# A smaller descriptor scratch for GpSimd, and four places instead of two at the start of the ring of expert weights

## The chip, the cores and the metric

The kernel runs on one core of a Trainium2 chip. A core has a matrix engine (TensorE, PE in the rows; its weight loads are PEld), a vector engine (VectorE, DVE), a scalar engine (ScalarE, ACT), a general engine (GpSimd, POOL), and a synchronisation engine (SyncE, SP) which here issues the DMA transfers. The engines run their own instruction queues in order and wait for one another by semaphores. All of them work on SBUF, an on-chip memory of 128 partitions; PSUM takes the results of TensorE. Times are device microseconds of one execution; lower is better.

## The reference

Two transformer blocks on 256 tokens of width 1024, all in fp32. The first has adaptive norms, a projection, Fourier mixing and neighbourhood attention, a gated merge and an MLP; the second has cross-attention to a memory, a convolution and a two-way RWKV7 recurrence, an output projection, and then the part which the change is named after, a feed-forward layer in which each of 16 experts chooses its 32 tokens:

```python
def expert_choice_ffn(h, w_router, w_gate, w_up, w_down):
    B, S, D = h.shape                                   # 1, 256, 1024
    cap = CAPACITY_FACTOR * S // N_EXPERTS              # 32 tokens an expert
    aff = jax.nn.softmax((h @ w_router).astype(jnp.float32), axis=-1)
    gates, idx = lax.top_k(jnp.swapaxes(aff, 1, 2), cap)
    xe = jax.vmap(lambda hb, ib: hb[ib])(h, idx)
    hid = jax.nn.silu(jnp.einsum('becd,edf->becf', xe, w_gate)) * jnp.einsum('becd,edf->becf', xe, w_up)
    ye = jnp.einsum('becf,efd->becd', hid, w_down) * gates[..., None].astype(h.dtype)
    bidx = jnp.arange(B)[:, None, None]
    return jnp.zeros_like(h).at[bidx, idx].add(ye)

def second_block(x, mem, ...):
    h = rms_norm_2(x, norm_mix_g)
    q, pc, pr = jnp.split(h @ w_in, [ATT_WIDTH, ATT_WIDTH + 2 * CONV_WIDTH], axis=-1)
    o_att, o_conv = memory_cross_attention(q, ...), conformer_conv(pc, ...)
    o_rwkv = rwkv7_bidirectional(pr, ...)
    x = x + jnp.concatenate([o_att, o_conv, o_rwkv], axis=-1) @ w_out
    x = x + expert_choice_ffn(rms_norm_2(x, norm_ffn_g), w_router, w_e_gate, w_e_up, w_e_down)
    return rms_norm_2(x, final_norm_g)
```

The experts' weights are 16 times three matrices of 1024 x 1024 fp32, 4 MB each, 192 MB in all.

## The kernel before

The tokens lie across the free axis, the features across the partitions. Weights of the two blocks come in pieces of 1024 KB: `wload` (L335, a DMA on SyncE) fetches one into a tile `raw`; `wsplit` makes from it a high part by a copy on ScalarE (L278) and a low part by a subtraction on VectorE (L284), both in the tile `split`; and TensorE multiplies the high and low parts of the activations (`hmh`, `hml` for the second block's input, `hxh`, `hxl` for the first's) with it into a PSUM tile `pw`. The helpers `mm` (L299), `tt` (L284), `ts` (L291, L293), `stt` (L296), `tp` (L287, GpSimd), `act` (L275) and `cpa` (L278) issue one instruction each, so that most rows carry one of these lines, and tiles are told apart by name.

The experts' weights go without a split. Each matrix is cut into four pieces of 1024 KB, with the very last one in five smaller ones (`LAST`), all in the order gate, up, down of expert 0, then of expert 1, and so on. They go through a ring of places of 8 KB per partition. `ring_room(n)` opens n places, `ring_load(n)` fetches the next n pieces of the list into the places which are free, and `used` gives a place back after its last matmul and loads again:

```python
    def ring_room(self, n):                                                        # L1869
        self.free.extend((self.pool(self.es, "ew", 1, "right"), "ew") for _ in range(n))
    def ring_load(self, n=1):                                                      # L1872
        for nm, e, q in itertools.islice(self.pieces, min(n, len(self.free))):
            ...
            with self.in_turn("SP"):
                self.nc.sync.dma_start(flat, w)                                    # L1886
            def used(slot, *piece):                                                # L2031
                ...
                    self.free.append(slot)
                    self.ring_load()
```

`in_turn` keeps the loads in program order on SyncE. Places are opened in five steps as earlier pools end, by the constants `RING, RING0, RING1, RING2, RING3` (L41): `RING` in `branches`, when the projection of the second block is done, RING0 = 10 and RING1 = 2 in the recurrence, RING2 = 4 before the router, RING3 = 1 in the experts. `GATHER` and `used` keep two pieces' places for other tiles.

`branches` computes the second block's convolution and recurrence, and the change's first step lies in it:

```python
        proj.close()                                                               # L1466
        ...
        self.ring_open()
        self.ring_room(RING)                                                       # L1470
        wk2, wk3 = (self.pool(early, n, 1, "right") for n in ("wk2", "wk3"))
        ...
        nc.sync.dma_start(sel, A["cr"][:, _CR["sel"]:])                            # L1476
        self.ring_load(RING)                                                       # L1477
```

`sel` is a table of 1 MB in the pool wk2. In wk3 lie the two tiles `xpad`, cleared on GpSimd (`memset`, L1545) and written by ScalarE. Near them, `start(d)` (L1429) prepares the recurrence for each direction: three `ts` on VectorE make `LM` from `aa` (L293), then follow `tt` and `stt` on `aa` and `ex`, and `tp` adds and products on GpSimd, and a copy `kds` there (L1444). TensorE's first matmuls on them are `psab<-xpad,aa`; its transposes `ptm` and products `pom` belong to the cross-attention. `experts` (L1939) gathers tokens (`pxe`), runs `gate_up` (`pgu`), and for each expert the down product (`pd`) and the sum (`acc`).

Two more names matter. `sumsq` (L476) squares activations on ScalarE (`sq`), adds them on GpSimd (`sa`, L287), and TensorE sums them over the partitions (`px<-ones,sa`). `qm` and `pad` are tiles cleared on GpSimd (L1253, L1282, L1283).

The order of the instructions on an engine is set by a scheduler from the dependences and the memory, except where `in_turn` fixes it. SBUF pools are two stacks, from the left and from the right; a tile in a new pool waits for the last use of whatever lay at its addresses. All transfers are issued by SyncE on hardware queues; GpSimd issues none.

Of the kernel before, what the change touches and what calls it, by code (L numbers as in the profile page):

```python
# [37 lines left out]
AH2 = 3  # L38
F1 = 0, 1, 2, 3
FILL = 28  # L40
RING, RING0, RING1, RING2, RING3 = 2, 10, 2, 4, 1  # L41

# [2154 lines left out]
```

## Time and profile before

| | us |
|---|---|
| median of 3 runs | 1192.12 (1191.79 to 1192.63) |
| profiled execution | 1191.58 |
| its span (first to last instruction) | 1189.8 |
| TensorE busy | 1074.5 (90%) |
| VectorE busy | 513.0 (43%) |
| ScalarE busy | 431.9 (36%) |
| GpSimd busy | 47.6 (4%) |
| DMA | 313.89 MB, mean 264 GB/s |
| ew pieces of 1024 KB | 64 gate, 64 up, 63 down, all on SyncE; median 19.9 us from issue to landing |

The rows below are of six views. The busy time by stage gives, for each stretch, its length, the busy time and number of instructions of PE, PEld, DVE, ACT and POOL, then the clock that TensorE was granted as a share of full speed, the busy share of the 16 DMA engines, and what they moved in GB/s. The chain of work that ended last is followed back from the last instruction; it is given in order of time as start, duration, work. The timeline of an engine gives start, duration, engine, line, operation, output<-inputs and sizes, number, and in brackets the idle time before it and what ended that. Equal neighbours are put together, with the duration from the first's start to the last's end. The waits give, for an engine and line, what was waited for, the total, the number and the longest. Times count from the start of the span; 1.78 us of the profiled execution lie outside it.

### The profile page before, as it was taken

The numbers are of one execution on the slowest core, as the hardware profiler recorded it, in microseconds if no ns is written. First come the engines' busy times: TensorE is split into PE (matmuls) and PEld (weight loads), VectorE is DVE, ScalarE is ACT, GpSimd is POOL, SyncE is SP. The second block draws the span as 40 slices with busy tenths as digits, with TensorE's granted clock in tenths as the row PEclk, the third lists the DMA queues.
The fourth block names the chain that finished last, engine by engine and source line by source line (L and its number), as shares of the span: only waits on it lengthen the run. The fifth ranks groups of instructions, "written<-read, shape, count | busy, mean of one in ns | idle before, by whom it ended". The sixth has DMA issues, their size and how long they took to land.

```text
span 1189.8 us, 19234 instructions
## 1 busy us (share of the span) xinstructions
PE 1074.5 (90%) x8140; PEld 758.5 (64%) x8140; DVE 513.0 (43%) x968; ACT 431.9 (36%) x742; POOL 47.6 (4%) x53
## 2 busy tenths in 40 slices
PE   5999999999999999998899998989977777877775
PEld 4886677799999999998578787434422222222222
DVE  3544455577655555759987546212111111111102
ACT  4541467657444444576554444101100000000003
POOL 0010000011000000101210002000000000000000
PEclk9999999999999999999799998999987888787888
DMA  9774545464555543521101368899999999999996
GB/s 357 291 275 155 177 155 194 182 240 146 212 195 191 177 178 111 207 108 36 72 1 46 142 269 358 355 419 420 418 421 418 420 419 418 420 419 421 418 420 273
DMA packets 46919, 313.89 MB, mean 264 GB/s; under 512 B 6128, under 2 KB 6896, under 8 KB 10480
## 3 DMA queue, kind: packets, MB, share of 16 engines
q1 hardware_dynamic: 46832, 312.66, 66.6%
q8 instruction: 64, 1.05, 0.4%
q14 instruction: 23, 0.19, 0.0%
HBM read 311.59 MB, written 1.05 MB: 263 GB/s over the span
## 4 chain that ended last, share of the span: by engine, by line
PE 62%; DMA 31%; DVE 2%; ACT 2%; POOL 1%; issue 1%; SPq 0%; ACTq 0%
PE pw L299 23%; DMA ew<-in_w_e_down_dram 12%; DMA ew<-in_w_e_up_dram 11%; PE acc L299 8%; DMA ew<-in_w_e_gate_dram 7%; PE pd L299 4%; PE pada L299 2%; PE pv L299 2%; PE psab L299 2%; PE pqf L299 2%; PE pgu L299 2%; PE py L299 1%; PE pg L299 1%; PE psc L299 1%; PE po L299 1%; DMA raw<-in_w_ada_dram 1%
## 5 line engine op out<-in xcount | busy, mean ns | idle before, releaser
L284 DVE TENSOR_TENSOR split<-raw,split 128x1024 fp32r<-128x1024 f32 (+2 forms) x148 | 176.7, 1203 | 114.0 <-ACT split L278 113.6
L278 ACT ACTIVATE split<-raw 128x1024 fp32r<-128x1024 f32 (+2 forms) x148 | 151.6, 1032 | 122.5 <-PE pw L299 64.5
L299 PE MATMUL pgu<-ew,XE 128*32 128x256 f32 x2048 | 149.2, 427 | 51.7 <-DMA ew<-in_w_e_up_dram 48.5
L299 PE MATMUL pd<-ew,hidT 128*32 128x512 f32 (+2 forms) x560 | 156.9, 603 | 9.5 <-DVE hidT L2093 7.8
L299 PEld LDWEIGHTS pgu<-ew,XE 128*32 128x32 f32 x2048 | 64.4, 119 | 127.8 <-DMA ew<-in_w_e_up_dram 74.6
L299 PEld LDWEIGHTS pd<-ew,hidT 128*32 128x32 f32 x560 | 41.3, 116 | 115.4 <-issue 99.4
L299 PE MATMUL acc<-uh,split 128*128 128x256 f32 x512 | 94.7, 283 | 0.0
L299 PE MATMUL pw<-h2h,split 128*128 128x256 f32 x512 | 92.9, 280 | 0.0
L296 DVE SCALAR_TENSOR_TENSOR hid<-pgu,rs,hid 128x256 f32<-128x256 f32 x16 | 7.7, 484 | 187.9 <-ACT hid L275 187.9
L296 DVE SCALAR_TENSOR_TENSOR ye<-pd,ig,ye 128x512 fp32r<-128x512 f32 (+2 forms) x35 | 24.6, 704 | 148.6 <-ACT ye L275 147.1
L275 ACT ACTIVATE hid<-pgu,rs 128x256 f32<-128x256 f32 x16 | 7.6, 473 | 213.3 <-PE pgu L299 213.3
L275 ACT ACTIVATE ye<-pd,ig 128x512 fp32r<-128x512 f32 (+2 forms) x35 | 22.8, 651 | 171.0 <-PE pd L299 170.9
L299 PEld LDWEIGHTS acc<-uh,split 128*128 128x128 f32 x512 | 80.8, 192 | 0.0
L299 PEld LDWEIGHTS pw<-h2h,split 128*128 128x128 f32 x512 | 79.2, 188 | 0.0
L299 PE MATMUL acc<-ul,split 128*128 128x256 f32 x256 | 72.5, 283 | 0.0
L299 PE MATMUL pw<-h2l,split 128*128 128x256 f32 x256 | 71.4, 279 | 0.0
L299 PE MATMUL pw<-hxh,split 128*128 128x256 f32 x320 | 61.6, 286 | 0.0
L299 PE MATMUL pw<-hmh,split 128*128 128x256 f32 x320 | 61.1, 288 | 0.0
L299 PEld LDWEIGHTS pw<-hxh,split 128*128 128x128 f32 x320 | 49.9, 188 | 8.6 <-issue 4.3
L299 PEld LDWEIGHTS pw<-hmh,split 128*128 128x128 f32 x320 | 50.6, 192 | 1.6 <-PE pz L299 0.5
L299 PEld LDWEIGHTS acc<-ul,split 128*128 128x128 f32 x256 | 49.0, 191 | 0.2 <-DVE ul L284 0.2
L299 PEld LDWEIGHTS pw<-h2l,split 128*128 128x128 f32 x256 | 48.0, 187 | 0.0
(444 smaller groups left out, 1788.9 us busy)
## 6 DMA issues: line engine op xcount, KB each, us to landing
ew<-in_w_e_gate_dram SPq DMA_DIRECT2D x64, 1024.0 KB, 19.9
ew<-in_w_e_up_dram SPq DMA_DIRECT2D x64, 1024.0 KB, 19.9
ew<-in_w_e_down_dram SPq DMA_DIRECT2D x63, 1024.0 KB, 19.9
raw<-in_w_mlp_dram SPq DMA_DIRECT2D x32, 1024.0 KB, 4.8
raw<-in_w_ada_dram SPq DMA_DIRECT2D x24, 1024.0 KB, 6.3
raw<-in_w_in_dram SPq DMA_DIRECT2D x18, 1024.0 KB, 4.9
raw<-in_w_branch_gate_dram SPq DMA_DIRECT2D x8, 1024.0 KB, 4.9
raw<-in_w_out_dram SPq DMA_DIRECT2D x4, 1024.0 KB, 5.8
```

Of the source, the lines that this page charges most:

```text
L275: self.nc.scalar.activation(out, in_, func, **kw)
L278: self.nc.scalar.activation(out, in_, AF.Copy)
L284: self.nc.vector.tensor_tensor(out=out, in0=a, in1=b, op=op)
L296: self.nc.vector.scalar_tensor_tensor(out=out, in0=a, scalar=s, in1=b, op0=op0, op1=op1)
L299: self.nc.tensor.matmul(out, lhsT, rhs, start=start, stop=stop, **kw)
```

## The change

The descriptor scratch which the program sets aside in SBUF for GpSimd is 16 KB per partition by default, and is set to 256 B. The constant `RING` goes from 2 to 4, so that two places of 8 KB more are opened at L1470, and four pieces are fetched at L1477.

```diff
-RING, RING0, RING1, RING2, RING3 = 2, 10, 2, 4, 1
+RING, RING0, RING1, RING2, RING3 = 4, 10, 2, 4, 1
@@
-    nc = bacc.Bacc("TRN2", target_bir_lowering=False, num_devices=1)
+    nc = bacc.Bacc("TRN2", target_bir_lowering=False, num_devices=1, dynamic_dma_scratch_size=256)
```

The left stack of pools ends 15.75 KB lower, the two new places lie below the two old ones on the right stack, and the pools wk2 and wk3, opened after them, lie 16 KB lower. ScalarE's order is unchanged, VectorE's but for one split that changes place with a `gate` product.

On SyncE, where the ring begins (`sel`, then `ew` pieces, with the last loads of `w_out` between them), lines with - of before, with + of after:

```order
 L1476 DMA sel<-in_cr_dram 128x2064
-L1886 DMA ew<-in_w_e_gate_dram 128x2048 x2
+L1886 DMA ew<-in_w_e_gate_dram 128x2048 x4
 L335 DMA raw<-in_w_out_dram 128x1280 x2
-L1886 DMA ew<-in_w_e_gate_dram 128x2048 x2
-L1886 DMA ew<-in_w_e_up_dram 128x2048 x2
+L1886 DMA ew<-in_w_e_up_dram 128x2048 x4
 L335 DMA raw<-in_w_out_dram 128x1280
```

Two more pieces go in front of the second block's `w_out`, and each later load of the ring fetches a piece two further on. Earlier on SyncE, two of four loads of the first block's `w_out` (128x2048, L335) move from behind `w_attn_out` to the place between a pair of `w_ada` and a `w_in`, and two small loads (`dup`, `w0b`) move to where these were.

On GpSimd, the same stage of the recurrence, with the semaphores that each instruction waits for (Activation is ScalarE), before:

```order
L287 TENSOR_TENSOR ex_5052<-pr,ex_5052 128x3x256 [waits DVE_49,Activation_49]
L287 TENSOR_TENSOR ex_5053<-pr,ex_5053 128x3x256 [waits Activation_49]
L1545 MEMSET xpad_5775 128x1024 [waits DMAHW4_49,DMAHW5_49,DMAHW3_49,DMAHW6_49,DMAHW2_49,DMAHW7_49,DMAHW1_49,DMAHW0_49]
L1545 MEMSET xpad_5776 128x1024 [waits DMAHW3_49,DMAHW6_49,DMAHW1_49,Activation_49]
L1444 COPY kds<-LM_5586 128x768 [waits DVE_49]
```

The same place after:

```order
L287 TENSOR_TENSOR ex_5052<-pr,ex_5052 128x3x256 [waits DVE_49,Activation_49]
L287 TENSOR_TENSOR ex_5053<-pr,ex_5053 128x3x256 [waits Activation_49]
L1545 MEMSET xpad_5785 128x1024 [waits DMAHW4_49,DMAHW3_49,DMAHW5_49,DMAHW2_49,DMAHW6_49,DMAHW1_49,DMAHW7_49,DMAHW0_49,PE_49]
L1545 MEMSET xpad_5786 128x1024 [waits DMAHW5_49,DMAHW4_49,DMAHW7_49,DMAHW2_49,DMAHW0_49]
L1444 COPY kds<-LM_5586 128x768 [waits DVE_49]
```

The order is the same, but the first memset of `xpad` has a wait for TensorE; the matmul it stands for is the last `pw<-hmh,split`, whose operand `hmh` lay at those addresses. `sel`, by the same shift, waits for a `pw<-hml` matmul instead of a split on VectorE.

On GpSimd, the row of `sa` adds between the two blocks (`qm` and `pad` are the cleared tiles):

```order
 L287 TENSOR_TENSOR sa<-sq 128x256
-L287 TENSOR_TENSOR sa<-sa,sq 128x256 x2
-L1253 MEMSET qm 128x1024
-L287 TENSOR_TENSOR sa<-sa,sq 128x256
-L1282 MEMSET pad_4845 128x2
-L1283 MEMSET pad_4845 128x2
-L1282 MEMSET pad_4846 128x2
-L1283 MEMSET pad_4846 128x2
-L287 TENSOR_TENSOR sa<-sa,sq 128x256
+L287 TENSOR_TENSOR sa<-sa,sq 128x256 x4
```

The five memsets go to the front of the three `gate` adds of the first block. On TensorE the matmul `px<-ones,sa` behind these adds stands six `pw` matmuls earlier.

## Rows read from the trace of the kernel before

**Rows 1.** Busy time by stage: recurrence and tail (columns as told above).
```profile
575.00:600.00 25.00, 24.44 (x107) 16.10 (x106) 22.57 (x44) 15.66 (x33) 4.84 (x4) 0.94 0.01 1
...
1100.00:1150.00 50.00, 37.13 (x290) 12.75 (x284) 4.11 (x9) 2.32 (x4) 0.00 (x0) 0.80 1.01 419
```

**Rows 2.** Chain in order of time: its last wait for expert weights.
```profile
1160.22 19.11 DMA ew<-in_w_e_down_dram
```

**Rows 3.** Timeline of PE in the tail: two groups of sixteen matmuls.
```profile
1132.77 1.07 PE L299 MATMUL pgu<-ew,XE 128*32 128x256 f32 x16 [1.43 <-DMA ew<-in_w_e_up_dram]
...
1140.25 1.93 PE L299 MATMUL pgu<-ew,XE 128*32 128x256 f32 x16 [0.56 <-DMA ew<-in_w_e_up_dram]
```

**Rows 4.** Timeline of SP: the first loads of the ring.
```profile
567.46 0.80 SPq L1886 DMA_DIRECT2D ew<-in_w_e_gate_dram  x2
```

**Rows 5.** Waits of SP, 540 to 780 us: its waits for one matmul.
```profile
SPq L1886 <- PE pgu L299: 23.9, 14, 11.0
```

**Rows 6.** Busy time by stage around the first expert's start.
```profile
740.00:745.00 5.00, 5.00 (x23) 3.51 (x25) 1.72 (x4) 0.47 (x1) 0.00 (x0) 0.50 0.63 257
745.70:757.20 11.50, 11.50 (x146) 6.83 (x143) 3.30 (x12) 3.09 (x5) 0.00 (x0) 1.00 0.85 323
```

**Rows 7.** Timeline of DVE: the first read of `sel`.
```profile
589.50 0.24 DVE L281 COPY Gc<-sel 128x192 f32<-128x192 f32 x1
```

**Rows 8.** Timeline of POOL, 557 to 569 us.
```profile
557.77 3.69 POOL L287 TENSOR_TENSOR ex<-pr,ex 128x768 f32<-128x768 f32 x2 [75.25 <-DVE stm L291]
561.41 1.84 POOL L1545 MEMSET xpad<- 128x1024 f32 x2
567.83 0.82 POOL L1444 COPY kds<-LM 128x768 f32<-128x768 f32 x1 [4.59 <-DVE LM L284]
```

**Rows 9.** Timeline of DVE: one scaling beside POOL's work, three without.
```profile
559.69 3.70 DVE L293 TENSOR_SCALAR LM<-aa,vec,oneka 128x256 f32<-128x256 f32 x1
...
570.97 1.05 DVE L293 TENSOR_SCALAR LM<-aa,vec,oneka 128x256 f32<-128x256 f32 x3
```

**Rows 10.** Chain in order of time, 558 to 576 us.
```profile
558.63 5.08 DVE LM L293 x3
...
567.48 2.24 PE pom L299 x8
...
571.68 3.75 PE psab L299 x4
```

**Rows 11.** Timeline of PE, 565 to 568 us.
```profile
565.92 1.09 PE L303 MATMUL ptm<-cm,smt 128*128 128x128 f32 x4 [3.92 <-DVE smt L291]
...
567.02 0.41 PE L299 MATMUL pw<-hmh,split 128*128 128x256 f32 x1
```

**Rows 12.** Timeline of ACT: its first write of `xpad`.
```profile
568.38 0.62 ACT L278 ACTIVATE xpad<-ex 64x512 f32<-64x512 f32 x1
```

**Rows 13.** Timelines of DVE, POOL and PE, 475 to 483 us.
```profile
475.09 0.49 DVE L296 SCALAR_TENSOR_TENSOR hml<-x,vec,hmh 128x256 fp32r<-128x256 f32 x1 [0.25 <-ACT hmh L275]
...
479.70 0.48 DVE L296 SCALAR_TENSOR_TENSOR hml<-x,vec,hmh 128x256 fp32r<-128x256 f32 x1 [0.19 <-ACT hmh L275]
...
479.63 0.95 POOL L1253 MEMSET qm<- 128x1024 f32 x1 [0.32 <-PE acc L299]
...
482.24 0.38 PE L299 MATMUL px<-ones,sa 128*128 128x1 f32 x2 [0.63 <-POOL sa L287]
```

**Rows 14.** Busy time by stage: twelve `pw` matmuls ahead of `px`.
```profile
480.20:481.60 1.40, 1.40 (x12) 1.20 (x11) 1.27 (x3) 1.40 (x4) 1.40 (x7) 1.00 0.00 0
```

**Rows 15.** Busy time by stage, near the start.
```profile
54.00:58.00 4.00, 3.98 (x28) 2.73 (x27) 3.44 (x5) 1.66 (x4) 0.00 (x0) 1.00 0.04 12
```

**Rows 16.** Timeline of ACT: splits behind loads of `w_in` and `w_out`.
```profile
63.43 1.05 ACT L278 ACTIVATE split<-raw 128x1024 fp32r<-128x1024 f32 x1
...
246.04 1.06 ACT L278 ACTIVATE split<-raw 128x1024 fp32r<-128x1024 f32 x1 [0.45 <-DMA raw<-in_w_out_dram]
```

**Rows 17.** Busy time by stage, behind the wait of rows 11.
```profile
565.00:570.00 5.00, 3.75 (x14) 2.57 (x14) 4.47 (x7) 2.21 (x6) 0.82 (x1) 0.50 0.27 84
```

## The prediction

> **What bounds the kernel now.** I read the busy time by stage first, since the shares of the whole span mix stages with different limits [rows 1]. In 575 to 600 us TensorE is busy 24.44 of 25 us while the DMA engines move 1 GB/s: there TensorE sets the time. In 1100 to 1150 us it is the other way about: the DMA engines are busy all the time at 419 GB/s, TensorE 37.13 of 50 us. The chain of work that ended last, in order of time, says what the end hangs on [rows 2]: the last piece of `down`, landing at 1160.22 + 19.11 = 1179.33. TensorE's own list in the tail says the same [rows 3]: sixteen `pgu` matmuls take 1.07 us, behind 1.43 us of waiting for their piece; at half the clock they take 1.93 us and the wait is 0.56, still above zero. A piece is 1024 KB, 1.0486 MB, so at 419 GB/s one takes 2.50 us, and the two lists agree: 1.07 + 1.43.
>
> The third thing to see is how the stream starts and what holds it before that. SyncE loads the first two pieces of the ring at 567.46 [rows 4]. Later it waits for places: of its waits from 540 to 780 us, 23.9 us in 14 times were for `pgu`, the matmuls that empty a place [rows 5]. In 740 to 745 us the engines therefore move only 257 GB/s [rows 6]; I call this the dip.
>
> **Two more places, −5.0 us.** Nothing that is computed goes away. Each release of a place still lets one load go, in the same order and after the same matmuls; only the piece that it fetches stands two further on in the list. The two pieces gained are fetched right behind the first two, after 567.46, where the queue has nothing else to do: in 575 to 600 us it moves 1 GB/s [rows 1]. `sel` goes in front of them and is first read at 589.50 [rows 7]; `sel` and four pieces are 5.25 MB, 12.5 us at 419 GB/s, so all are in at about 580. From then on, through the dip, the stream is two pieces ahead at every point, and the tail, which is nothing but stream, ends two pieces earlier: 2 × 2.50 = 5.0 us. I price a piece by the full rate, since the pieces drop out of the saturated stretch. What is late next is TensorE, but it idles 1.43 us in each 2.50 us of stream at full clock and 0.56 at half [rows 3], so it follows.
>
> **The two `xpad` memsets, −1.85 us.** This is a side effect of addresses. In before, GpSimd adds `ex` twice (3.69 us from 557.77), clears `xpad` twice (1.84 us from 561.41) and copies `kds` at 567.83 [rows 8]. Beside it VectorE scales `LM` three times; the second takes 3.70 us, from 559.69 to 563.39, where three undisturbed ones take 1.05 us together [rows 9]. It ends right behind the second memset (563.25), so I read that the second add and both memsets hold it. That is on the path: the chain stands on `LM` for 5.08 us, with `pom` and `psab` behind [rows 10]. In the changed kernel the pool of `xpad` lies lower, over an old operand of `pw`, so the first memset also waits for TensorE's last `pw<-hmh` matmul. That one runs at 567.02, after `ptm` at 565.92 [rows 11], which itself waits for VectorE's work behind `LM`. So `LM` comes in after the second add, 1.84 us earlier, and with it `ptm`, `pom` and `psab`.
>
> What now hangs on the memsets: `pw<-hmh` would end at 567.02 + 0.41 − 1.84 = 565.6, the memsets at 566.5 and 567.4. GpSimd's copy of `kds` queues behind them and starts no later than 567.83. ScalarE's first write of `xpad` is at 568.38 [rows 12], 566.54 after the shift, at or just behind the end of the first memset: 0 to +0.9 if it needs the second. VectorE does two-input work in that time; how this fares beside a memset is seen at 480 us, where the memset of `qm` covers an `hml` of 0.48 us, against 0.49 us without one [rows 13]. So I take nothing back, −1.85. It stays to the end, because TensorE is full from there on (24.44 of 25 us) and its `pgu` matmuls release the places in the dip.
>
> The Trainium skill, in "SBUF — State Buffer", "Who interferes with whom", says that VectorE and GpSimd share one port pair, that whoever has it holds it for the whole instruction, and that the other is blocked until then. If it is handed over at the end of each instruction, `LM` comes in behind the second add, at 561.46, and the memsets cost nothing; the row of 3.70 us, which runs past both memsets, speaks against that. By that rule the sum would be −4.7; the same result is rival B.
>
> **The other moves.** `px`: the memset of `qm` (0.95 us at 479.63) and four small ones leave GpSimd's row of `sa` adds for an earlier place; TensorE had waited 0.63 us for the last add before `px` at 482.24 [rows 13]. In the new order `px` stands six `pw` matmuls earlier, 0.70 us of work (12 of them in 1.40 us [rows 14]), so part of what lay before it lies behind. The adds are freed of about 1 us, but not the squares by ScalarE that feed them, so I take `px` as ready about 0.4 earlier, at 481.85. It then saves 0.4 of waiting and puts 0.70 us of matmuls behind: +0.3. Bounds: −0.6 (the adds are done when TensorE comes there, and the wait is gone) and +0.7 (they are done no earlier than before); I keep the value between, nearer to the upper.
>
> `w_out`: two loads of 1024 KB go from about 240 us to about 50 us, in front of one of `w_in` at 57 us. The DMA engines stand nearly idle for 4 us there (12 GB/s in 54 to 58 us [rows 15]); the two take 5.0 us, so `w_in` lands 1 to 2 us later, at about 62, and the next split of a weight is at 63.43 [rows 16]. Cost 0; if that cover is gone, +1.0. At 246 ScalarE had waited 0.45 us for `w_out`: at best −0.45. `sel` now waits for a matmul and not for a split by VectorE, with 9 us to spare: 0. One split of VectorE changes place with a `gate` product: 0.
>
> **The sum** against the profiled execution, 1191.58 us: 1191.58 − 5.0 − 1.85 + 0.3 = 1185.0. The median before stands 0.54 above the profiled one, so the forecast is **1185.6 us**. The measurement can tell about 0.2%, 2.4 us: faster is below 1189.7, slower above 1194.5.
>
> **The rivals.** A is the forecast, 1185.6: 0.55.
>
> B: the memsets did not hold `LM`, or the 1.85 us are lost again (ScalarE's write waits for them): −4.7, 1187.4. For: there is one instance only. Against: the 3.70 us end 0.14 us after the second memset. 0.14.
>
> C, the clock: TensorE stands 3.92 us ahead of `ptm` [rows 11], and in 565 to 570 us its granted clock is 0.50, the lower of the two levels (1.2 of 2.4 GHz) [rows 17]; there `pom` takes 2.24 and the first `psab` 3.75 us [rows 10]. If with 1.84 us less of idling the clock does not fall, these halve: −1.1 − 1.9 = −3.0 more, 1182.6. For: the idle time is halved. Against: half of it is left. 0.19.
>
> D: the two extra pieces give nothing, because the stream is held at the dip by something other than places; the rest is −1.55, 1190.6. Against: the waits for `pgu` [rows 5]. 0.05.
>
> E, the slower one: TensorE's clock in the dip. It is 0.50 in 740 to 745 us and 1.00 in 745.7 to 757.2 [rows 6], the 11.5 us in which TensorE, busy throughout, gathers tokens, runs the first expert's `pgu` and so releases the places. At half clock sixteen `pgu` take 1.93 against 1.07 us [rows 3], 1.8 times as long. Should the clock come back only after this stretch, it is 11.5 × 0.8 = +9.2 us: **1194.8**. It decides from the point where 5 of the 11.5 us run at half clock, which takes the forecast past 1189.7, and all of them make it slower than before. Against: nothing on TensorE changes its order there, and the whole stage comes 1.5 us earlier as one. 0.04.
>
> F, the change does not do what it says because 256 B is too little: any issue on SyncE beyond 2.50 us per piece would stretch the tail. Against: all 191 full pieces are issued by SyncE, none by GpSimd. It would be slower by an amount that no row bounds: 0.03.
>
> **How the numbers follow.** A, B and C are faster: 0.88. D, and E with half of its stretch, are the same: 0.07. The rest of E, and F, are slower: 0.05. The range takes in C's 1182.6, with `w_out`'s −0.45 below it, and B's 1187.4, with `w_out`'s +1.0 above it: **1182.2 to 1188.6**.
>
> **What the changed profile would show.** Four issues of the ring behind `sel`, and a rate in 575 to 580 us far above 1 GB/s; the last piece landing some 6.5 us before 1179.33; the tail still at 418 to 421 GB/s. The long `LM` at about 1.9 us, the memsets behind the last `pw<-hmh`, at about 565.6, `ptm` at about 564.1 plus what the stage before lost or won. A wait of near 1 us before `px` in its new place. I would be wrong if the memsets turned up on the path again, if the clock differed at 565 or 745, or if the rate in the dip fell by what the two pieces gave.

## The result, and the profile after

| | us |
|---|---|
| before, 3 runs shown, profiled one | 1192.12, 1191.58 |
| before, beside the changed kernel, 6 runs | 1191.29 |
| changed, median of 6 runs (lowest, highest) | 1185.18 (1183.66, 1187.67) |
| changed, profiled execution, its span | 1184.47, 1182.7 |
| ratio to before, 95% interval | 0.9950, 0.9938 to 0.9961 |
| changed, five more runs, ratio | 1184.68, 0.9944 (0.9931 to 0.9958) |

The forecast was 1185.6 us, faster; the interval of the ratio lies wholly below 1, so it is faster, by 0.5%. The two profiled executions differ by 7.1 us. To see where, I cut both at five marks that stand in either trace: the first `sa` add on GpSimd between the two blocks, the first `LM` on VectorE, `ptm` on TensorE, the first load of the second block's `w_out` on SyncE, and the long group of the first expert's `pgu` in the chain; the last stretch goes to the end of the span. The rows of the marks in the kernel before, of five views (GpSimd's and VectorE's timelines, SyncE's timeline, the chain; start and duration first; `ptm` is in [rows 11]):

```profile
475.66 0.74 POOL L287 TENSOR_TENSOR sa<-sq 128x256 f32<-128x256 f32 x1 [193.08 <-ACT sq L275]
...
558.54 5.17 DVE L293 TENSOR_SCALAR LM<-aa,vec,oneka 128x256 f32<-128x256 f32 x3
...
640.34 2.73 SPq L335 DMA_DIRECT2D raw<-in_w_out_dram  x2
...
753.56 3.62 PE pgu L299 x62
```

The same marks in the changed kernel:

```profile
475.65 0.74 POOL L287 TENSOR_TENSOR sa<-sq 128x256 f32<-128x256 f32 x1 [193.08 <-ACT sq L275]
...
559.25 3.41 DVE L293 TENSOR_SCALAR LM<-aa,vec,oneka 128x256 f32<-128x256 f32 x3
...
564.87 1.06 PE L303 MATMUL ptm<-cm,smt 128*128 128x128 f32 x4 [2.16 <-DVE smt L291]
...
639.16 2.72 SPq L335 DMA_DIRECT2D raw<-in_w_out_dram  x2
...
751.75 3.62 PE pgu L299 x62
```

Differences of these, and of the same rows in the traces of the experiments below, give the ledger (us; one trace each):

| kernel | start to `sa` | `sa` to `LM` | `LM` to `ptm` | `ptm` to `w_out` | `w_out` to `pgu` | `pgu` to end |
|---|---|---|---|---|---|---|
| before | 475.66 | 82.88 | 7.38 | 74.42 | 113.22 | 436.24 |
| changed | 475.65 | 83.60 | 5.62 | 74.29 | 112.59 | 430.95 |
| changed, again | 477.08 | 83.61 | 5.62 | 73.98 | 112.91 | 430.90 |
| e1_scratch_only | 475.53 | 83.60 | 7.39 | 74.30 | 114.85 | 436.73 |
| e4_room_unused | 474.83 | 83.60 | 5.62 | 73.95 | 113.18 | 436.12 |
| e2_three_places | 477.50 | 83.61 | 5.62 | 73.96 | 112.96 | 434.05 |
| e6_load_two | 474.81 | 83.60 | 5.62 | 73.97 | 113.05 | 432.45 |
| e7_qm_later | 475.63 | 83.59 | 7.39 | 74.41 | 113.71 | 436.77 |
| e8_sq_first | 474.53 | 82.36 | 5.61 | 73.59 | 112.49 | 431.82 |

The changed kernel against before: 0.0, +0.72, −1.76, −0.13, −0.63, −5.29, together −7.1. The last column is good to 0.05 us, since a span is given to 0.1. The first column lies anywhere between 474.5 and 477.5 us, and 1.4 us apart in the two executions of the changed kernel alone, so single traces are compared by stretches here. A stretch, too, can move by the moment of an execution: between `sa` and `LM` the traces of e3 and e11 (not in the table) have 84.37 and 84.38 us, since the granted clock fell there to 0.66 and 0.68 in 485 to 490 us, where the other twelve have 1.00.

The stages, as in [rows 1, 6, 15, 17], columns as there:

```profile
54.00:58.00 4.00, 3.98 (x27) 2.73 (x27) 3.44 (x6) 1.87 (x4) 0.00 (x0) 1.00 0.99 334
...
575.00:600.00 25.00, 23.88 (x108) 15.94 (x107) 22.68 (x48) 16.02 (x34) 3.81 (x3) 1.00 0.22 91
1100.00:1150.00 50.00, 40.63 (x252) 14.26 (x256) 5.60 (x11) 3.70 (x6) 0.00 (x0) 0.83 1.01 420
740.00:745.00 5.00, 5.00 (x39) 3.79 (x39) 1.80 (x4) 0.62 (x2) 0.00 (x0) 0.76 0.43 165
```

The tail is still the stream, at 420 GB/s. In 575 to 600 us the mean is 91 GB/s where it was 1: this is the end of the four pieces. In 54 to 58 us, where 12 GB/s went, the two `w_out` pieces run at 334. The dip at 740 is there as before: in 740 to 745 us the rate is lower, 165 against 257 GB/s, but over 740 to 750 us it is 265 against 238, so the dip has moved within that time and is no deeper.

SyncE's timeline, then the chain's last transfer, to set against [rows 4, 2]:

```profile
566.18 0.33 SPq L1476 DMA_DIRECT2D sel<-in_cr_dram  x1
566.63 2.21 SPq L1886 DMA_DIRECT2D ew<-in_w_e_gate_dram  x4
```

```profile
1153.59 18.64 DMA ew<-in_w_e_down_dram
```

Four issues stand behind `sel`, at 0.55 us each, and the chain's last piece lands at 1172.23, 7.1 us earlier than before.

GpSimd, VectorE and TensorE around the `xpad` memsets, to set against [rows 8, 9, 11]:

```profile
558.48 3.71 POOL L287 TENSOR_TENSOR ex<-pr,ex 128x768 f32<-128x768 f32 x2 [75.96 <-DVE stm L291]
566.42 1.84 POOL L1545 MEMSET xpad<- 128x1024 f32 x2 [4.24 <-PE pw L299]
568.21 0.82 POOL L1444 COPY kds<-LM 128x768 f32<-128x768 f32 x1
...
560.40 1.93 DVE L293 TENSOR_SCALAR LM<-aa,vec,oneka 128x256 f32<-128x256 f32 x1
...
565.95 0.41 PE L299 MATMUL pw<-hmh,split 128*128 128x256 f32 x1
```

The memsets wait 4.24 us for TensorE's `pw` and begin when its last `pw<-hmh` ends, at 566.36. The second `LM` takes 1.93 us in place of 3.70 and ends at 562.33, 0.14 us behind the second `ex` product.

### The profile page after: what moved, and what is told of

It reads as the page before. It is cut to its first block, busy times and chain, and to the rows that moved or that the text cites. A ratio compares the mean times of both kernels' runs of the same rounds, so it can differ in the third digit from the quotient of the medians.

```text
span 1182.7 us, 19224 instructions
## 1 busy us (share of the span) xinstructions
PE 1069.1 (90%) x8140; PEld 755.8 (64%) x8140; DVE 511.0 (43%) x968; ACT 431.9 (37%) x742; POOL 47.9 (4%) x53
## 4 chain that ended last, share of the span: by engine, by line
PE 62%; DMA 30%; DVE 4%; ACT 2%; POOL 1%; issue 1%; SPq 0%; ACTq 0%; DVEq 0%; POOLq 0%
PE pw L299 23%; DMA ew<-in_w_e_up_dram 10%; DMA ew<-in_w_e_down_dram 10%; PE acc L299 9%; DMA ew<-in_w_e_gate_dram 8%; PE pd L299 3%; PE pgu L299 2%; PE pv L299 2%; PE pada L299 2%; PE py L299 1%; PE pg L299 1%; PE psc L299 1%; PE po L299 1%; PE pp L299 1%; PE psab L299 1%; PE pqf L299 1%
## 5 line engine op out<-in xcount | busy, mean ns | idle before, releaser
L299 PE MATMUL pgu<-ew,XE 128*32 128x256 f32 x2048 | 152.6, 435 | 48.7 <-DMA ew<-in_w_e_up_dram 42.5
L299 PE MATMUL pd<-ew,hidT 128*32 128x512 f32 (+2 forms) x560 | 151.6, 591 | 8.9 <-DVE hidT L2093 7.7
```

The source lines that it names most:

```text
L299: self.nc.tensor.matmul(out, lhsT, rhs, start=start, stop=stop, **kw)
```

## The experiments

All are compared with the kernel before, run on the same chip in between; "same chip" figures of before lie between 1191.3 and 1192.0.

### The ring and the memsets, taken apart

**e1_scratch_only** keeps the scratch of 256 B and gives the room to nobody:

```diff
-RING, RING0, RING1, RING2, RING3 = 4, 10, 2, 4, 1
+RING, RING0, RING1, RING2, RING3 = 2, 10, 2, 4, 1
```

> The scratch is 256 B, but the ring starts with two places as before. Theory: the scratch alone gives nothing; the xpad memsets stay at their old place, so the long LM stays at 3.7 us, and px, six matmuls earlier, costs 0.7 us, so the time is 0.7 above the kernel before, 1192.0 against 1191.3, with ptm at about 566.6. Rival (the gain is in the scratch or in the earlier w_out loads, not in the ring): 1185 to 1188.

Measured: 1193.53 us, ratio 1.0013 (1.0003 to 1.0022), so 1.8 us above before and not 0.7. `px` has the wait of the changed kernel, 1.35 us. The second `LM` on VectorE and the memsets on GpSimd are the old ones:

```profile
560.29 3.71 DVE L293 TENSOR_SCALAR LM<-aa,vec,oneka 128x256 f32<-128x256 f32 x1
...
562.01 1.84 POOL L1545 MEMSET xpad<- 128x1024 f32 x2
```

The ledger gives the 0.72 of `px`, and 1.6 us between `w_out` and `pgu`. The trace shows where these lie: TensorE waits 0.44 and 0.70 us at `pw<-orw,split` (719.4 and 720.4), which it does not in the kernel before; VectorE does a split of a `w_out` piece there ahead of the `kds` products that `orw` is made from. In this kernel SyncE's row has one piece of `down` ahead of a `gate` piece and the `w_out` loads elsewhere among the ring's; I put the 1.6 us down to that, but it was not tried alone. The scratch itself gives nothing, and neither do the early `w_out` loads, which are in this kernel too.

**e4_room_unused** has every address of the changed kernel, but the two new places stay empty:

```diff
-        self.ring_room(RING)
+        self.ring_room(2)
+        for n in range(2):
+            self.pool(self.es, "un", 1, "right").tile([128, 2048], F32, tag="un", name="un", bufs=1)
```

> As the changed kernel, with all its addresses, but the two new places are left empty: two pieces are loaded at the start. Theory: memsets late, LM block 3.3 us, ptm at 564.9 as in the changed kernel, and the last piece lands 5.0 us later, at about 1177.2: 1190.2 us. Rival (the extra places do nothing, and all comes from the head): 1185.2.

Measured: 1189.89 us, 0.9982 (0.9972 to 0.9992); the forecast was 1190.2. `LM` to `ptm` is 5.62 us as in the changed kernel, `pgu` to the end 436.12 as in the one before. The late memsets are a matter of addresses, the 5 us at the end one of the places.

**e2_three_places** is the changed kernel with `RING = 3`.

> Scratch 256 B, three places. Theory: one piece is worth 2.5 us; the first memset waits for a late pw matmul here too, so the head is that of the changed kernel: 1187.7 us, last landing at about 1174.7. Rival (only the first extra place counts, or only both together): 1185.2 or 1190.2.

Measured: 1187.40 us, 0.9964 (0.9950 to 0.9978). The last stretch is 434.05: one place is worth some 2.2 us, two are worth 5.3. Traces with two places lie between 435.6 and 436.8, so the third place's 2.2 and the 2.50 that I priced are not told apart. A cleaner measure is the time from the `pgu` mark to the landing of the last `ew` piece: 426.2 to 427.0 us in the eight traces with two places (427.0 in the kernel before), 424.5 with three, and 421.5 to 422.1 in the five with four (421.7 in both traces of the changed kernel). By the means one place is worth 2.2 us and two 4.9.

**e6_load_two** has four places and fills two of them late:

```diff
-        self.ring_load(RING)
+        self.ring_load(2)
```

> The changed kernel with its four places, but only two pieces are loaded behind sel; the other two places are filled by the later loads of the ring. Theory: what counts is how far ahead the stream is at the dip, and the queue has room for two pieces before that: 1185.2 us, last landing as in the changed kernel. Rival (the idle time at 570 to 600 us is what is used, and nothing later can replace it): 1190.2.

Measured: 1187.34 us, 0.9959 (0.9946 to 0.9972). By the medians that lies between the two theories, but the interval overlaps those of the changed kernel, and the trace is of the fastest of the five executions, 1185.27 us. Its last stretch is 432.45, 1.5 us more than in the changed kernel. Busy time in 710 to 720 us, of the changed kernel and of this one:

```profile
710.00:720.00 10.00, 10.00 (x82) 9.82 (x82) 9.32 (x15) 4.45 (x7) 0.00 (x0) 1.00 0.67 238
```

```profile
710.00:720.00 10.00, 10.00 (x81) 9.85 (x80) 8.98 (x15) 4.84 (x7) 0.00 (x0) 1.00 1.01 419
```

The two late pieces fill the hole that the changed kernel leaves at 710 us, and both fit: the last `ew` load is issued at 1155.41, 404.36 us behind the `pgu` mark at 751.05, where the changed kernel has 404.65. Its landing follows the mark by 421.5 us, against 421.7. SyncE's last loads, and the busy time in the 3.5 us up to that landing, first of the changed kernel, then of e6:

```profile
1146.11 10.29 SPq L1886 DMA_DIRECT2D ew<-in_w_e_down_dram  x5
...
1170.00:1173.50 3.50, 2.92 (x41) 1.88 (x41) 2.29 (x6) 2.39 (x11) 0.00 (x0) 1.00 0.29 118
```

```profile
1145.14 10.27 SPq L1886 DMA_DIRECT2D ew<-in_w_e_down_dram  x5
...
1169.00:1172.50 3.50, 3.50 (x37) 1.89 (x29) 1.52 (x4) 1.67 (x6) 0.00 (x0) 0.52 0.30 122
```

The 1.5 us of the trace come behind the stream. TensorE's granted clock is 0.52 there, in place of 1.00, while it runs the last expert's `down`; it is busy throughout instead of waiting for a piece, and from the last landing to the end of the span it takes 11.0 us instead of 9.2. So in this trace the queue has room for both pieces, and the idle time at 570 us can be replaced. Why the clock is low at that moment, and whether it is so in the other four executions, the record does not show.

### `px`

**e7_qm_later** is the kernel before, with the memset of `qm` behind the `sa` adds. TensorE's row changes in one place: `px` stands six matmuls earlier, as in the changed kernel.

```diff
-        nc.gpsimd.memset(qm, 0.0)
+        with self.in_turn("Pool"):
+            nc.gpsimd.memset(qm, 0.0)
```

> The kernel before with the memset of qm behind the sa adds. The scheduler then puts px six matmuls earlier, as in the changed kernel, and nothing else of weight moves. Theory: the adds end where they ended, px starts where it started, and 0.7 us of matmuls come behind it: 1192.4 us against 1191.7, LM 0.72 us later. Rival (the last adds end earlier without the memset): px 0.4 to 0.6 us earlier and the time at 1191.7.

Measured: 1192.57 us against 1191.96, 1.0004 (0.9994 to 1.0013): no difference by that interval. The trace has what the times can't tell: `px` starts where it did, and `LM` comes 0.71 us later.

```profile
482.21 0.38 PE L299 MATMUL px<-ones,sa 128*128 128x1 f32 x2 [1.35 <-POOL sa L287]
```

Why the adds end no earlier is seen on GpSimd's timeline, the last two adds of before (the first of them behind the `qm` memset of [rows 13]), then the same two of the changed kernel:

```profile
480.55 0.74 POOL L287 TENSOR_TENSOR sa<-sa,sq 128x256 f32<-128x256 f32 x1
...
481.38 0.80 POOL L287 TENSOR_TENSOR sa<-sa,sq 128x256 f32<-128x256 f32 x1
```

```profile
480.38 0.74 POOL L287 TENSOR_TENSOR sa<-sa,sq 128x256 f32<-128x256 f32 x1 [1.06 <-ACT sq L275]
...
481.19 0.98 POOL L287 TENSOR_TENSOR sa<-sa,sq 128x256 f32<-128x256 f32 x1
```

The first of the two waits for ScalarE's square as I said, but it was held by the `qm` memset by only 0.17 us in before (480.55 against 480.38), not by one. The second starts 0.19 us earlier and takes 0.98 us in place of 0.80, so it ends at 482.17, against 482.18. Beside it VectorE runs an `hml` product with two inputs in SBUF, which ends at 481.60 in before and at 481.59 in the changed kernel; in both, and in e7, the add ends 0.58 us behind it. That the `hml` product holds the add would fit this, but it was not tried.

**e8_sq_first** is the changed kernel with the matmuls of `px` in another order, so that TensorE does not come to the add first:

```diff
-            part = (self.part.pop(id(ps)), sq[:, 0], sq[:, 1])
+            part = (sq[:, 0], sq[:, 1], self.part.pop(id(ps)))
```

> The changed kernel, with the products px in another order: the two squares first, the sum sa last, so that TensorE no longer stands before px. Theory: the 1.35 us of waiting there go, with at most 0.45 us of it coming back as a wait for the last squares; this passes through to the end: 1184.1 us (1183.8 to 1184.3) against 1185.2. Rival (the wait is hidden by something later): 1185.2.

Measured: 1184.88 us (5 runs), 0.9938 (0.9924 to 0.9952). The wait is gone, and the stretch to `LM` is 1.24 us shorter than in the changed kernel, 82.36. But its median is that of the changed kernel. In its trace, the fastest of the five executions (1182.14 us), the last stretch is 0.9 us longer (431.82 against 430.9); the stream is not behind, its last piece lands 421.9 us after the mark against 421.7, and 0.7 of the 0.9 us come behind that landing, as in e6. Whether the 1.24 us reach the end, the times of five runs don't decide.

### What holds VectorE at `LM`

The forecast held that GpSimd keeps VectorE waiting through several instructions on end. Three kernels, each the one before with another cut of the memsets:

**e3_memset_twice** issues each memset twice.

```diff
+            nc.gpsimd.memset(t, 0.0)
             nc.gpsimd.memset(t, 0.0)
```

> The kernel before with each xpad memset issued twice, 1.84 us more of GpSimd's work behind the ex products. Theory: VectorE's second LM is held until the last of four memsets ends, 3.70 + 1.84 = 5.5 us, ptm moves from 565.92 to 567.8, and the whole kernel is 1.8 us longer, 1193.1. Rival (handed over at the end of each GpSimd instruction): LM stays at 3.7 us or less and the time at 1191.3.

Measured: 1193.18 us, 1.0014 (1.0001 to 1.0027), near the forecast, but not by its way. The scheduler put the second pair behind the `kds` copy, `LM` stayed at 3.71 us, and `psab` was late instead, since it needs `xpad`: ScalarE's write right before it ends 6.19 us behind `ptm`, and 5.67 in before. Of these 0.5 us 0.24 are left at `w_out`. The largest difference of this trace from before is the clock between `sa` and `LM`, 1.49 us, so what makes the ten runs longer stays open. The run says nothing on the question.

**e9_memset_pieces** and **e11_memset_pieces_again** are one program, with memsets of a quarter, six of eight right behind the `ex` products; **e10_memset_halves** has halves (its loop is over `t[:, z]`), three of four there.

```diff
-            nc.gpsimd.memset(t, 0.0)
+            for z in [t[:, a, b] for a in range(2) for b in range(2)]:
+                nc.gpsimd.memset(z, 0.0)
```

> The kernel before with each xpad memset cut into four of a quarter of its columns; six of the eight pieces stand right behind the ex products, two behind the kds copy. Theory: VectorE stays held as long as GpSimd has one instruction behind another, whatever their number, so the second LM lasts until the sixth piece ends, 3.3 to 3.7 us, and ptm comes at most 0.4 us earlier: 1191.3 to 1191.7. Rival (the pair is handed over at the end of an instruction): LM ends behind the first small piece, at 2.2 us, and ptm comes 1.5 us earlier: 1190.2.

> The kernel before with each xpad memset cut into two halves; three stand right behind the ex products, the fourth behind kds. In e9_memset_pieces quarters let VectorE through (LM block 3.47 us). If GpSimd's memset holds VectorE only while one long instruction follows another at once, halves lie between: theory (length of the instruction decides): LM block 4.3 to 4.9 us; rival (any cut lets VectorE in): 3.5 us; third (the quarters were an accident of the moment): 5.2 us.

> The kernel of e9_memset_pieces once more, for a second trace, since its time did not follow its trace. Theory (VectorE gets in between small pieces): LM block 3.5 us again, LM to ptm 5.7. Rival (accident of one execution): LM block 4.9 to 5.2, ptm 7.0 to 7.4 behind its start.

First a row that all of these kernels share with the one before, VectorE's first `LM` and the first `ex` product, here in before:

```profile
558.54 1.23 DVE L293 TENSOR_SCALAR LM<-aa,vec,oneka 128x256 f32<-128x256 f32 x1
...
557.77 1.84 POOL L287 TENSOR_TENSOR ex<-pr,ex 128x768 f32<-128x768 f32 x1 [75.25 <-DVE stm L291]
```

VectorE's second `LM` and GpSimd's row, in e9, e11 and e10 in this order:

```profile
560.72 1.93 DVE L293 TENSOR_SCALAR LM<-aa,vec,oneka 128x256 f32<-128x256 f32 x1
...
558.80 3.69 POOL L287 TENSOR_TENSOR ex<-pr,ex 128x768 f32<-128x768 f32 x2 [75.26 <-DVE stm L291]
562.44 1.86 POOL L1546 MEMSET xpad<- 128x256 f32 x6
```

```profile
561.40 3.44 DVE L293 TENSOR_SCALAR LM<-aa,vec,oneka 128x256 f32<-128x256 f32 x1
...
559.48 3.71 POOL L287 TENSOR_TENSOR ex<-pr,ex 128x768 f32<-128x768 f32 x2 [76.75 <-DVE stm L291]
563.13 1.57 POOL L1546 MEMSET xpad<- 128x256 f32 x6
```

```profile
559.25 3.32 DVE L293 TENSOR_SCALAR LM<-aa,vec,oneka 128x256 f32<-128x256 f32 x1
...
560.98 1.44 POOL L1546 MEMSET xpad<- 128x512 f32 x3
```

In e11 `LM` ends at 564.84, 0.14 us behind the sixth piece, and in e10 at 562.57, 0.15 behind the third half: one `LM` waits through an `ex` product and three or six memsets, whatever their size. In e9, the same instructions in another execution, VectorE got in behind the product (562.65), and it was GpSimd that lost time, 1.86 us for six pieces in place of 1.57. So the theory holds for the second `LM` in e11 and e10 and falls in e9. As a rule for any row of GpSimd's it fails in every trace: the first `LM` ends 0.15 to 0.16 us behind the first `ex` product (559.77 against 559.62 in before), although the second product follows at once, and so it is in all thirteen traces that have these products on GpSimd. What the traces show is narrower. Between two products VectorE got in each time; between the second product and memsets that follow at once it got in once (e9) and waited for the last of them six times (before, e1, e3, e7, e10, e11). Whether it is the kind of the next instruction that decides was not tried, and why e9 differs from e11 stays open. The times, 1192.11 us for e9 (1.0005, 0.9995 to 1.0014), 1191.62 for e10 (0.9996, 0.9985 to 1.0008) and 1194.22 for the one run of e11, whose trace has the low clock behind `sa`, show no gain. e9's trace is of the fastest of its ten executions (1190.08 us), which fits that it is an exception and does not prove it.

### The changed kernel again, and a faster one

**a2_after_again** is the changed kernel, for a second trace.

> The changed kernel once more, beside f2_products_moved on the same chip, for a second trace. Theory: 1185.2 us; from the first sa add to LM 83.6 us, LM block 3.3 to 3.4 us, LM to ptm 5.6 us, as in the first trace; the clock in the dip may fall at another moment by up to 0.7 us. Rival (the first trace was a lucky one in these rows too): LM block near 5.2.

Measured: 1184.68 us, 0.9944. All stretches between the marks agree with the first trace within 0.05 us but two that hang on the clock (below).

**f2_products_moved** is e8 with the `ex` products on VectorE and the `LM` scalings on ScalarE:

```diff
-P1 = (1, 0, 0), (1, 1, 0)
+P1 = (0, 0, 0), (0, 1, 0)
@@
-                self.ts(kd[:, i], aa[d][:, i], self.v("k_a_2", i), ALU.mult, oneka[:, i:i + 1], ALU.add)
+                self.act(kd[:, i], aa[d][:, i], AF.Identity, scale=self.v("k_a_2", i), bias=oneka[:, i:i + 1])
```

> The kernel of e8_sq_first with two more edits, to free VectorE at the LM block: the two ex products go from GpSimd to VectorE (0.87 us each), and the six LM scalings from VectorE to ScalarE, which stands idle there for 5 us. Theory: VectorE is no longer held by GpSimd; from the start of the block to ptm it takes 3.4 us instead of 5.6, and since TensorE waits for it there, 1.5 to 2.2 us of this reach the end: 1182.7 to 1183.4 against 1184.9. Rival (VectorE is full from 570 to 588 us anyway and now has one product more): 1184.9.

Measured: 1180.39 us (4 runs), 0.9909 (0.9894 to 0.9925), 4.3 us below the changed kernel on the same chip, better than both theories. VectorE's, ScalarE's and TensorE's rows:

```profile
558.04 0.95 DVE L284 TENSOR_TENSOR ex<-pr,ex 128x768 f32<-128x768 f32 x1
...
559.49 1.58 ACT L275 ACTIVATE LM<-aa,oneka,vec 128x256 f32<-128x256 f32 x3
...
561.21 0.63 PE L303 MATMUL ptm<-cm,smt 128*128 128x128 f32 x4
562.31 1.35 PE L299 MATMUL pom<-pTm,vm 128*64 128x256 f32 x8
```

A product that took GpSimd 1.85 us takes VectorE 0.95, `ptm` has no wait at all, and TensorE's clock does not fall before `pom`, which takes 1.35 us, not 2.15 to 2.24 (the granted clock is 1.00 in 560 to 565 us, and 0.80 in 565 to 570, where before has 0.50). From `sa` to `ptm` its trace wins 3.7 us against the changed kernel, 1.24 of them e8's. The last stretch is 1.2 us longer, 0.9 of it behind the last landing, as in e6. The two edits at `LM` were not tried apart. It is the best kernel of this study.

## Why the prediction was right, point by point

**Two more places, −5.0.** Measured 5.3 in the last stretch (436.24 to 430.95; 430.90 in the second trace). e4 shows that it is the places, e2 that one gives about half. The price by the full rate was right: to the last landing the two places are worth 5.3 us in this pair of traces and 4.9 by the means of all. What the text left out lies behind that landing: it is 9.2 us to the end of the span in before, in both traces of the changed kernel and in e3, with a granted clock of 1.00 in the 3.5 us up to the landing, and 9.6 to 11.0 in the other ten traces, with 0.52 to 0.96. That the profiled pair agrees there is luck.

**The `xpad` memsets, −1.85.** Measured −1.76: 5.61 or 5.62 in every trace with the late memsets and the products on GpSimd, 7.38 or 7.39 in every one with whole memsets at the early place. `pw<-hmh` ended at 566.36, 0.7 later than said, which is `px`'s delay; ScalarE's first write of `xpad` came just in time behind the first memset:

```profile
567.41 0.63 ACT L278 ACTIVATE xpad<-ex 64x512 f32<-64x512 f32 x1
```

The first memset ended at 567.37. `kds` started at 568.21 and not "no later than 567.83". In the second trace the chain even lists the memsets and `kds`, up to 570.32; but ScalarE's second write of `xpad`, which comes behind `om` and `vv`, ends there at 571.52, right before `psab` at 571.61, and `psab` stands 5.30 us behind `ptm` where it stood 5.76 before, so they cost nothing. Rival B is out on both its ways for this row of GpSimd's. Its port rule is the Trainium skill's in "SBUF — State Buffer", "Who interferes with whom": whoever issues first has the shared pair for the whole instruction, and the other is blocked. Read as a hand-over at the end of each instruction, it agrees with the first `LM` in every trace (0.15 us behind one product) and with the second in e9. In e11, e10, the kernel before and e1, e3 and e7 the second `LM` waits through several instructions.

**`px`, +0.3.** This is the term that was mis-sized: +0.72. The step that failed is "I take `px` as ready about 0.4 earlier"; it was ready at the same time, 482.23 against 482.24, so the upper bound, +0.7, was the right value. I had counted the length of the memset taken out, 0.95 us, and not what it really held up, 0.17, and even that was lost in the add behind it.

**`w_out`, `sel`, the rest, 0.** `sa` starts at 475.65 against 475.66, so the early loads cost nothing. The cover was thinner than I said: ScalarE's split, at 63.43 in [rows 16], now waits 0.47 us for `w_in`, and the wait of the next, 1.19 us before, is shorter for it:

```profile
64.21 1.06 ACT L278 ACTIVATE split<-raw 128x1024 fp32r<-128x1024 f32 x1 [0.47 <-DMA raw<-in_w_in_dram]
65.88 1.06 ACT L278 ACTIVATE split<-raw 128x1024 fp32r<-128x1024 f32 x1 [0.61 <-PE pw L299]
```

**The clock, rivals C and E.** C happened in part, and its price was wrong. TensorE stood 2.16 us ahead of `ptm`, not 3.92. In the second trace `ptm` still ran at full clock, 0.63 us where it took 1.09, and `pom` and `psab` at the lower one:

```profile
566.31 0.63 PE L303 MATMUL ptm<-cm,smt 128*128 128x128 f32 x4 [2.16 <-DVE smt L291]
...
567.41 2.24 PE L299 MATMUL pom<-pTm,vm 128*64 128x256 f32 x8
```

That is −0.44 in the stretch to `w_out`. In the first trace the clock had fallen by `ptm` (1.06), was back for the first two `psab` (1.10 us together) and low again for the next two (2.04); a stage of [rows 17] has 0.67 where it had 0.50. I had put 1.9 us on that, and it gave 0.13, because the chain then goes over VectorE:

```profile
565.00:570.00 5.00, 3.50 (x14) 2.38 (x13) 3.79 (x6) 3.46 (x9) 2.61 (x3) 0.67 0.57 178
```

```profile
569.80 1.05 DVE LM L293 x3
570.85 2.35 DVE vv L296 x2
573.20 2.48 DVE aa L284
```

The price of C was worked out on TensorE's rows alone, without asking what is late next. E's mechanism was there with the other sign: from `w_out` to `pgu` the mean granted clock is 0.97 in both traces of the changed kernel and 0.95 in before, and the stretch is 0.63 and 0.31 us shorter. e4, with the changed kernel's addresses, has 0.95 and −0.04, and e9, with those of before, has 0.97 and −0.37, so this is the moment of an execution rather than the change.

**D and F** are out: e4 against the changed kernel is D's answer, and four issues in 2.21 us, with the tail at 420 GB/s, are F's.

The sum came out right, 1185.18 against 1185.6, and in part by luck. `px` was 0.4 too cheap and the clock's 0.75 (both traces) not counted: two errors against each other. And the forecast started from 1192.12, the median of three runs of before; against the 1191.29 of six the gain is 6.1 us, where 6.55 were forecast.

## What to carry to other kernels

Room in SBUF that a program holds for something it never does is worth what it buys at the bound of the kernel, here some 2.5 us for each 8 KB per partition; whether it buys anything is read at the stages before the bound, where the stream must have idle time to use it (here at 570 us, or as in e6 at 710). A change of addresses also moves waits: look at what each new tile lay over, since here a third as much came from two memsets that had to wait. And price a freed wait by what the waiting work still waits for: a wait counts only what it holds up (0.17 us of a memset of 0.95), and a faster stage only until the next engine is late.

## What the runs showed of the hardware

VectorE's `LM`, 0.35 us in a row of three alone, waited up to 3.4 us behind back-to-back work of GpSimd, through one product and two, three or six memsets; the same program once let it in behind the product (e9, e11). Between two products on end it got in each time, in thirteen traces. The same product takes GpSimd 1.85 us and VectorE 0.95. A transfer of 1 MB takes 2.50 us of the saturated queue, 419 to 421 GB/s, with two, three or four places at the start alike. With all pieces landed the end took 9.2 to 11.0 us, longest (e6) where TensorE's granted clock was 0.52 up to the last landing. The changed kernel came to the first common mark at 475.65 us in one execution and at 477.08 in another.
